# Rotary tables computed on folded tiles and spread through DRAM, with the softplus held in its place

## The chip, the cores and the metric

The kernel runs on one core of a Trainium2 chip. The metric is the device time of one execution in microseconds. The engines are named as in the profile: PE (matrix multiply; PEld is its weight load), DVE (vector), ACT (scalar functions and copies), POOL (not used here), SP (here it only issues DMAs). SBUF is the core's own memory with 128 partitions, PSUM holds the results of PE.

## The reference, cut to what matters

One layer of an encoder with 256 tokens and a model width of 2048. The normed input goes through one large projection. Its columns feed a latent attention (MLA) and a state space branch (SSD); both are gated, summed, projected, and followed by a gated feed-forward part. Two small pieces matter here: the rotary tables of the attention, and the softplus that makes the step sizes of the SSD.

```python
def rope_tables(positions):
    half = QK_ROPE_DIM // 2                      # 32 frequencies
    inv_freq = ROPE_THETA ** (-jnp.arange(half, dtype=jnp.float32) / half)
    ang = positions.astype(jnp.float32)[..., None] * inv_freq
    return jnp.cos(ang), jnp.sin(ang)

def apply_rope(x, cos, sin):
    x1, x2 = jnp.split(x.astype(jnp.float32), 2, axis=-1)
    return jnp.concatenate([x1 * cos - x2 * sin, x1 * sin + x2 * cos], axis=-1).astype(x.dtype)
...
    q_rope = apply_rope(q_rope, cos[:, :, None, :], sin[:, :, None, :])
    k_rope = apply_rope(k_rope, cos, sin)
...
    dt = jax.nn.softplus(dt_raw.astype(jnp.float32) + dt_bias.astype(jnp.float32))
```

## The kernel before

Activations lie with channels on the 128 partitions and the 256 tokens along the free axis. All projections are one list of jobs. A job multiplies a slab of 16 weight blocks (128 x 128 each, `raw`, three buffers, loaded by SP) with an activation. To keep float32 precision each half slab of 8 blocks is split in two: ACT makes the rounded part `wh` (L151), DVE the rest `wl` (L152), with five buffers each, so that the halves are made up to five ahead of PE (`HB=5`). PE multiplies `wh` with both parts of the activation in one matmul of 512 columns (L178, or L213 to L215 in jobs that give tokens on the partitions) and `wl` with the large part in 256 columns (L185).

The jobs at the start are: four slabs of the query latent `q` and four of the key/value latent `kv`, which use the unnormed input; then `kr` (the rotary key, from `krf`) and `dt` (the raw step sizes, `dtv`), which use the normed input `nHL` (tiles named xHL too, made in four quarters by `emit_n`: L314 on DVE scales, L290 on ACT and L291 on DVE split); a gate unit (L213 to L215, tiles `gate`); `R0` (the rotary part of the queries, from the normed latent `latH`/`latL`; matmuls L157 to L159); three gate units; `V0` (values, L573 to L575); `QK0`, and so on through the attention.

Small work is hung on the jobs by slot number with `at(slot, function)`. `rope_tables` is a generator whose steps are drawn a few at a time from slot 5 to 13. It computes, for all 128 partitions (each frequency four times, since the partitions hold two heads of two halves) and all 256 tokens, the angle, a long reduction of it to less than one turn (operations L337, L338, L341 in chains), the sine and the cosine (ACT, L366 and L367), and a sign by partition for the sine (L370). `swapped` exchanges the two halves of each head with four DMAs between SBUF tiles (`sw`, L377, issued by ACT), and `rotate` forms the rotated vector (L382 to L384). This happens once for `krf` and for each half of `R0` and `R1` (`rf`). `dt_softplus` is hung on slot 41. Of its instructions only the first, `nea` (L445), is kept in program order; the others may be moved earlier by the scheduler.

A scheduler of the tile framework sets the final order of each engine's instructions; each engine then runs its own list in order, and waits on semaphores. A DMA stands in the list of the engine that issues it. DMAs of SP and ACT count their completions on eight counters that the program hands out in turn: a DMA first waits until the earlier one on its counter has landed.

Of the kernel before, what the change touches and what calls it, by code (L numbers as in the profile page):

```python
# [8 lines left out]
F32 = mybir.dt.float32  # L9
F32R = mybir.dt.float32r  # L10
I32 = mybir.dt.int32
AF = mybir.ActivationFunctionType
ALU = mybir.AluOpType
AX = mybir.AxisListType

P = 128
S = 256
# [17 lines left out]
C_ID, C_U, C_L, C_INVF, C_SGN = 0, 128, 256, 384, 385  # L35
# [24 lines left out]
def tile_bidir_hybrid_layer(ctx: ExitStack, tc, xT, pos, vec, cst, w_in, w_r, w_v, w_qk, w_oa,  # L60
                            w_os, w_out, w_up, w_dn, out, RAWB=3, HB=5, NPG=29, NP1=18):
    nc = tc.nc
# [5 lines left out]
    dr = ctx.enter_context(tc.tile_pool(name="dr", bufs=1, space=bass.MemoryType.DRAM))  # L68

    act, dve, pe = nc.scalar, nc.vector, nc.tensor  # L70
# [4 lines left out]
    def p1(shape=(P, S), dt=F32, name="p1"):  # L75
        return pp.tile(list(shape), dt, tag="p1", bufs=NP1, name=name)
# [12 lines left out]
    CT = cp.tile([P, NCONST], F32, name="CT")  # L89
# [13 lines left out]
    def vcol(name, i=0):  # L103
        o = VOFF[name] + i
        return V[:, o:o + 1]
# [213 lines left out]


    rot = {}

    def rope_tables():

        cosT = rot["c"] = p1(name="cosT")
        sinT = rot["s"] = p1(name="sinT")
        pi_ = p1(dt=I32, name="posi")
        nc.scalar.dma_start(pi_, pos.broadcast_to([P, S]))
        a = p1(name="ang")
        q = p1(name="angq")  # L330
        qh = p1(name="angqh")
        t = p1(name="angt")
        k = p1(name="angk")
        MAGIC = 12582912.0

        def rounded(dst, src, scale):
            yield dve.tensor_scalar(dst, src, scale, MAGIC, ALU.mult, ALU.add)  # L337
            yield dve.tensor_scalar(dst, dst, MAGIC, None, ALU.subtract)  # L338

        def add_scaled(dst, src, c):  # L340
            yield dve.scalar_tensor_tensor(dst, src, c, dst, ALU.mult, ALU.add)  # L341

        def less_turns():
            yield from rounded(k, a, float(np.float32(1.0 / (2 * np.pi))))
            for c in TURN:
                yield from add_scaled(a, k, -c)


        yield dve.tensor_copy(a, pi_)
        yield dve.tensor_scalar(a, a, CT[:, C_INVF:C_INVF + 1], None, ALU.mult)  # L350
        yield from rounded(q, a, 2.0 ** -12)
        yield from add_scaled(a, q, -2.0 ** 12)
        yield from rounded(qh, q, 2.0 ** -10)
        yield from add_scaled(q, qh, -2.0 ** 10)
        yield dve.tensor_scalar(t, qh, TURN22[0], None, ALU.mult)
        yield from add_scaled(t, q, TURN12[0])
        yield from rounded(k, t, 1.0)
        yield dve.tensor_sub(t, t, k)
        yield from add_scaled(t, q, TURN12[1])
        yield from add_scaled(t, qh, TURN22[1])  # L360
        yield from less_turns()
        yield from add_scaled(a, t, 2 * float(np.pi))
        yield from less_turns()
        lim = float(np.nextafter(np.float32(np.pi), np.float32(0)))
        yield dve.tensor_scalar(a, a, lim, -lim, ALU.min, ALU.max)
        act.activation(sinT, a, AF.Sin)  # L366
        yield act.activation(cosT, a, AF.Sin, scale=0.5)  # L367
        yield dve.tensor_mul(cosT, cosT, cosT)
        yield dve.tensor_scalar(cosT, cosT, -2.0, 1.0, ALU.mult, ALU.add)
        yield dve.tensor_scalar(sinT, sinT, CT[:, C_SGN:C_SGN + 1], None, ALU.mult)  # L370

    def swapped(q, nb):

# [69 lines left out]
    def dt_softplus():  # L443
        v = dts["v"]
        tc.keep_in_program_order(act.activation(nea, vcol("alog"), AF.Exp))  # L445
        e, t, t2, o = p1(name="e"), p1(name="t"), p1(name="t2"), p1(name="o")
        act.activation(e, v, AF.Abs)
        act.activation(e, e, AF.Exp, scale=-1.0)
        dve.tensor_scalar(t, e, 2.0, None, ALU.add)
        dve.reciprocal(t, t)  # L450
        dve.tensor_mul(t, t, e)
        dve.tensor_mul(t2, t, t)
        n = 9
        dve.tensor_scalar(o, t2, 2.0 / (2 * n + 1), 2.0 / (2 * n - 1), ALU.mult, ALU.add)
        for k in range(n - 2, -1, -1):
            dve.tensor_mul(o, o, t2)
            dve.tensor_scalar(o, o, 2.0 / (2 * k + 1), None, ALU.add)
        dve.tensor_mul(o, o, t)
        dve.scalar_tensor_tensor(o, v, 0.0, o, ALU.max, ALU.add)
        dts["dt"] = o  # L460
        a = p1(name="a")
        dve.tensor_scalar(a, o, nea, -1.0, ALU.mult, ALU.mult)
        dts["a"] = a
# [525 lines left out]
    def at(slot, fn, *a):  # L989
        late.append((slot, lambda: fn(*a)))  # L990
# [14 lines left out]
    at(10, lat_norm, "kv")  # L1005
    at(13, lat_norm2, "kv", "kvn")
    steps = rope_tables()

    def rope_steps(n):
        for _ in range(n):  # L1010
            next(steps, None)

    for m in range(5, 14):
        at(m, rope_steps, 4 if m < 13 else 99)
    at(14, kr_rope)
    at(41, dt_softplus)
    at(46, dt_tokens)
    at(48, dt_cumsum)
# [67 lines left out]
    for g in range(G):  # L1086
# [9 lines left out]
        e, f = len(jobs) - b, 1  # L1096
# [205 lines left out]
```

## Time and profile before

| what | value |
|---|---|
| median of 3 runs | 1962.59 us (1961.36 to 1962.71) |
| the profiled execution | 1962.68 us, of which 1960.9 us from the first to the last instruction |
| PE busy | 1945.8 us (99%) |
| DVE busy | 1444.6 us (74%) |
| ACT busy | 1205.3 us (61%) |
| granted clock of PE | 0.998 |

In a timeline row the columns are start and duration in us, engine, line, operation, output and inputs, count, and in brackets the idle time of the engine ahead of it with what ended that. "x4" after a row means four instructions in a run, the duration being that of all. A row of `ACTq` or `SPq` is an instruction that only the engine's queue handles, such as the issue of a DMA. In the rows that group by line, the columns are the count, the busy time and the mean in ns of one, and the idle time before them.

### The profile page before, as it was taken

Reading aid. Unit: us, or ns where it says so; the run is one execution under the profiler, and the core shown is the slowest. Engines: PE = TensorE matmul, PEld = TensorE weight load, DVE = VectorE, ACT = ScalarE, POOL = GpSimd, SP = SyncE. Lnnn points to the kernel's source line nnn. Section 1 sums busy time; section 2 is a strip of 40 time slices with the busy share of each in tenths; the row PEclk is TensorE's granted clock in tenths of the full one; section 3 lists DMA queues with packets and bytes.
Section 4 is the critical chain, followed back from the end, with each engine's and each line's share of the span. In section 5 each row is a group of like instructions: output and inputs, shape, how many; then the busy total and the mean of one; then the engine's idle time right before and its main releaser. Section 6 shows DMA issues by size and latency. Waiting matters only on the chain.

```text
span 1960.9 us, 28920 instructions
## 1 busy us (share of the span) xinstructions
PE 1945.8 (99%) x11136; PEld 1707.2 (87%) x11136; DVE 1444.6 (74%) x2349; ACT 1205.3 (61%) x1878; POOL 0.2 (0%) x4
## 2 busy tenths in 40 slices
PE   9999999999999999999999999999999999999997
PEld 8889988888888888888888888888888888888887
DVE  7897744779779789879755566777656777557775
ACT  6566544687887887978644455666435655346553
POOL 0000000000000000000000000000000000000000
PEclk9999999999999999999999999999999999999999
DMA  7554456765665565565666665555555555555543
GB/s 279 179 173 154 137 172 216 251 222 172 215 233 173 198 234 194 194 215 182 205 196 198 200 222 176 190 193 192 181 189 190 194 192 175 194 192 193 188 161 124
DMA packets 93259, 379.31 MB, mean 193 GB/s; under 512 B 10688, under 2 KB 11328, under 8 KB 62912
## 3 DMA queue, kind: packets, MB, share of 16 engines
q1 hardware_dynamic: 91440, 375.09, 56.6%
q10 hardware_dynamic: 1680, 2.37, 0.4%
q8 instruction: 87, 1.43, 0.3%
q14 instruction: 52, 0.43, 0.1%
HBM read 371.91 MB, written 4.33 MB: 192 GB/s over the span
## 4 chain that ended last, share of the span: by engine, by line
PE 95%; DVE 3%; DMA 1%; ACT 1%; issue 0%; ACTq 0%; DVEq 0%; SPq 0%
PE g L178 42%; PE g L185 22%; PE g L214 7%; PE g L213 7%; PE g L215 7%; PE g L159 1%; PE g L157 1%; PE g L158 1%; DVE wl L152 1%; PE s L789 1%; PE s L798 1%; PE s L158 0%; PE s L159 0%; PE s L157 0%; PE s L771 0%; PE s L634 0%
## 5 line engine op out<-in xcount | busy, mean ns | idle before, releaser
L152 DVE TENSOR_TENSOR wl<-raw,wh 128x1024 fp32r<-128x1024 f32 (+1 forms) x670 | 802.7, 1209 | 328.1 <-ACT wh L151 181.3
L151 ACT ACTIVATE wh<-raw 128x1024 fp32r<-128x1024 f32 (+1 forms) x670 | 698.9, 1047 | 546.6 <-PE g L178 352.0
L178 PE MATMUL g<-xHL,wh 128*128 128x512 f32 x1424 | 341.7, 392 | 1.3 <-DVE xHL L291 1.1
L178 PE MATMUL g<-hHL,wh 128*128 128x512 f32 x1360 | 324.8, 391 | 0.0
L178 PEld LDWEIGHTS g<-xHL,wh 128*128 128x128 f32 x1424 | 262.4, 188 | 53.6 <-DVE xHL L291 1.5
L178 PEld LDWEIGHTS g<-hHL,wh 128*128 128x128 f32 x1360 | 249.8, 188 | 48.3
L185 PEld LDWEIGHTS g<-xHL,wl 128*128 128x128 f32 x1424 | 182.6, 191 | 7.0
L185 PE MATMUL g<-xHL,wl 128*128 128x256 f32 x1424 | 184.9, 283 | 0.0
L185 PEld LDWEIGHTS g<-hHL,wl 128*128 128x128 f32 x1360 | 174.3, 191 | 6.6
L185 PE MATMUL g<-hHL,wl 128*128 128x256 f32 x1360 | 176.4, 283 | 0.0
L178 PE MATMUL g<-aHL,wh 128*128 128x512 f32 x692 | 166.6, 391 | 0.1
L910 DVE SCALAR_TENSOR_TENSOR uc<-u,V,uc 128x255 f32<-128x255 f32 x176 | 85.3, 485 | 88.4 <-ACT uc L908 85.3
L178 PEld LDWEIGHTS g<-aHL,wh 128*128 128x128 f32 x692 | 126.9, 188 | 25.6 <-DVE aHL L928 1.3
L213 PE MATMUL g<-wh,yHL 128*128 128x512 f32 x256 | 100.1, 391 | 0.0
L214 PE MATMUL g<-wl,xHL 128*128 128x512 f32 x256 | 100.0, 391 | 0.0
L213 PE MATMUL g<-wh,xHL 128*128 128x512 f32 x256 | 100.0, 391 | 0.0
L215 PE MATMUL g<-wh,yHL 128*128 128x512 f32 x256 | 99.7, 389 | 0.0
L215 PE MATMUL g<-wh,xHL 128*128 128x512 f32 x256 | 99.6, 389 | 0.0
L214 PE MATMUL g<-wl,yHL 128*128 128x512 f32 x256 | 99.6, 389 | 0.0
L185 PEld LDWEIGHTS g<-aHL,wl 128*128 128x128 f32 x692 | 89.2, 191 | 3.6
L185 PE MATMUL g<-aHL,wl 128*128 128x256 f32 x692 | 90.4, 283 | 0.0
L684 DVE SCALAR_TENSOR_TENSOR xs<-cu,V,xs 128x254 f32<-128x254 f32 (+1 forms) x128 | 59.0, 479 | 0.2
(298 smaller groups left out, 2534.1 us busy)
## 6 DMA issues: line engine op xcount, KB each, us to landing
raw<-in_w_in SPq DMA_DIRECT2D x88, 1024.0 KB, 4.9
raw<-in_w_up SPq DMA_DIRECT2D x88, 1024.0 KB, 4.8
raw<-in_w_in SPq DMA_DIRECT2D x128, 256.0 KB, 3.9
raw<-in_w_os SPq DMA_DIRECT2D x128, 256.0 KB, 3.6
raw<-in_w_dn SPq DMA_DIRECT2D x32, 1024.0 KB, 5.0
raw<-in_w_oa SPq DMA_DIRECT2D x64, 256.0 KB, 3.9
FB<-acsD SPq DMA_DIRECT2D x32, 512.0 KB, 7.4
raw<-in_w_out SPq DMA_DIRECT2D x14, 1024.0 KB, 5.0
```

Source lines behind the costliest of these rows:

```text
L151: act.activation(vh, r, AF.Copy)
L152: dve.tensor_sub(vl, r, f32(vh))
L157: pe.matmul(ps, lhsT=wH, rhs=xH, start=first, stop=False)
L158: pe.matmul(ps, lhsT=wH, rhs=xL, start=False, stop=False)
L159: pe.matmul(ps, lhsT=wL, rhs=xH, start=False, stop=last)
L178: pe.matmul(ps, lhsT=wh[:, b, :], rhs=x, start=k == 0, stop=False)
L185: pe.matmul(cell["ps"][:, 0, :], lhsT=wl[:, b, :], rhs=get(k)[:, 0, :], start=False, stop=k == ktot - 1)
L213: pe.matmul(ps, lhsT=x[:, 0, ts], rhs=wH[:, kk, :], start=k == 0, stop=False)
L214: pe.matmul(ps, lhsT=x[:, 0, ts], rhs=wL[:, kk, :], start=False, stop=False)
L215: pe.matmul(ps, lhsT=x[:, 1, ts], rhs=wH[:, kk, :], start=False, stop=k == kt - 1)
L684: dve.scalar_tensor_tensor(o[:, a], u[:, b], vcol("cw", k * 48 + cb), o[:, a], ALU.mult, ALU.add)
L910: dve.scalar_tensor_tensor(o[:, a], u[:, b], vcol("fcw", k * 88 + cb), o[:, a], ALU.mult, ALU.add)
```

## The change

The tables are computed once per angle. There are 32 frequencies and 256 tokens; they are folded on the 128 partitions as four groups of 32 frequencies with 64 tokens each, so each operation has 64 columns instead of 256. Four DMAs load the positions of the four groups. The results (`tr`, cosine and sine) are stored with four DMAs in a DRAM tile `rotD` of 32 x 2 x 256 and loaded back with eight, four for the cosine table and four for the sine table, each to 32 partitions. The sign is applied to the sine after that, on 256 columns. The steps are drawn eight at a time from slot 5 to 10. The first operation of the softplus itself is also kept in program order.

```diff
     rot = {}
+    rotD = dr.tile([32, 2, S], F32, name="rotD")
 
     def rope_tables():
-        cosT = rot["c"] = p1(name="cosT")
-        sinT = rot["s"] = p1(name="sinT")
-        pi_ = p1(dt=I32, name="posi")
-        nc.scalar.dma_start(pi_, pos.broadcast_to([P, S]))
-        a = p1(name="ang")
...
-        k = p1(name="angk")
+        pi_ = p1((P, 64), I32, name="posi")
+        w = p1((P, 4, 64), name="ang")
+        a, q, qh, t = (w[:, i, :] for i in range(4))
+        k = p1((P, 64), name="angk")
+        tr = p1((P, 2, 64), name="trig")
+        cosT, sinT = tr[:, 0, :], tr[:, 1, :]
+        for c in range(4):
+            nc.scalar.dma_start(pi_[32 * c:32 * c + 32], pos[:, 64 * c:64 * c + 64].broadcast_to([32, 64]))
...
         yield dve.tensor_scalar(cosT, cosT, -2.0, 1.0, ALU.mult, ALU.add)
-        yield dve.tensor_scalar(sinT, sinT, CT[:, C_SGN:C_SGN + 1], None, ALU.mult)
+        for c in range(4):
+            nc.scalar.dma_start(rotD[:, :, 64 * c:64 * c + 64], tr[32 * c:32 * c + 32])
+        for i, nm in enumerate("cs"):
+            rot[nm] = p1(name="rot")
+            for c in range(4):
+                nc.scalar.dma_start(rot[nm][32 * c:32 * c + 32], rotD[:, i, :])
+        yield dve.tensor_scalar(rot["s"], rot["s"], CT[:, C_SGN:C_SGN + 1], None, ALU.mult)
...
-        act.activation(e, v, AF.Abs)
+        tc.keep_in_program_order(act.activation(e, v, AF.Abs))
...
-    for m in range(5, 14):
-        at(m, rope_steps, 4 if m < 13 else 99)
+    for m in range(5, 11):
+        at(m, rope_steps, 8 if m < 10 else 99)
```

The scheduler's order changes in three places; line numbers of the changed kernel are one higher than before up to the end of the tables and seven higher after them. Outside the first 110 us and the softplus, all engines keep their order.

First, ACT's list around the copy of the rotary key `krf`, before:

```order
L290 ACTIVATE xHL<-xw 128x512 x2
L151 ACTIVATE wh<-raw 128x1024
L237 ACTIVATE krf<-g 128x256
L377 DMA sw<-krf 32x256 x4
L419 ACTIVATE r_q<-s 128x256
L151 ACTIVATE wh<-raw 128x4x2x128
L439 ACTIVATE dtv<-g,V 128x256
L151 ACTIVATE wh<-raw 128x4x2x128
L424 ACTIVATE latH<-q 128x1024
L259 ACTIVATE rtok<-u,epsc 128x1 x2
```

and after:

```order
L372 DMA rotD<-trig 64x1x64 x4
L151 ACTIVATE wh<-raw 128x4x2x128
L376 DMA rot<-rotD 32x256 x8
L237 ACTIVATE krf<-g 128x256
L151 ACTIVATE wh<-raw 128x4x2x128
L384 DMA sw<-krf 32x256 x4
L426 ACTIVATE r_q<-s 128x256
L446 ACTIVATE dtv<-g,V 128x256
L259 ACT_TABLE_LOAD
L259 ACTIVATE rtok<-u,epsc 128x1
L431 ACTIVATE latH<-q 128x1024
```

The sine and cosine, with their table load, now come ahead of this piece (before, they stood behind it, between the DMAs of `rf`), the stores and loads of the tables stand ahead of the copy of `krf`, and a table load for the square root stands ahead of `rtok`.

Second, DVE's list from the last `kv` slab to the quarters of the normed input, before:

```order
L238 TENSOR_TENSOR kv<-kv,g 128x256
L314 TENSOR_TENSOR xw<-xw,r_x 128x1024
L402 TENSOR_TENSOR kvs<-kvs,sq_614 128x256
L314 TENSOR_TENSOR xw<-xw,r_x 128x1024
L291 TENSOR_TENSOR xHL<-xw,xHL 128x512 x2
L358 TENSOR_TENSOR angt<-angt,angk 128x256
L291 TENSOR_TENSOR xHL<-xw,xHL 128x512 x2
```

and after:

```order
L291 TENSOR_TENSOR xHL<-xw,xHL 128x512
L338 TENSOR_SCALAR angk<-ang 128x64
L409 TENSOR_TENSOR kvs<-kvs,sq_626 128x256
L339 TENSOR_SCALAR angk<-angk 128x64
L314 TENSOR_TENSOR xw<-xw,r_x 128x1024
L342 SCALAR_TENSOR_TENSOR ang<-angk,ang 128x64
L152 TENSOR_TENSOR wl<-raw,wh 128x4x2x128
L291 TENSOR_TENSOR xHL<-xw,xHL 128x512 x2
```

The last step before `krf` is one of the last reduction now (L342 with `angk`), where it was the middle of the first (L358); and the low half `wl` of the first gate unit stands ahead of the last quarter, where it stood behind it.

Third, DVE's list between the tables and `latL`, the small part of the query latent, after (before, these scalings of `q` by L422 stood among table steps, and the products of `krf` behind `latL`):

```order
L152 TENSOR_TENSOR wl<-raw,wh 128x4x2x128
L377 TENSOR_SCALAR rot<-rot,CT 128x256
L429 SCALAR_TENSOR_TENSOR q<-q,V,r_q 128x256 x4
L447 TENSOR_TENSOR dtv<-dtv,g 128x256
L389 TENSOR_TENSOR sw<-sw,rot 128x256
L390 TENSOR_TENSOR krf<-krf,rot 128x256
L391 TENSOR_TENSOR krf<-krf,sw 128x256
L432 TENSOR_TENSOR latL<-q,latH 128x1024
```

The sign on the loaded sine now stands ahead of the scalings of `q`, and the rotation of `krf` ahead of `latL`. The softplus, which stood on DVE among the first attention heads, now stands among the jobs of the attention's output projection.

More of the change, by code (lines that the diff above doesn't have):

```diff
@@ L321, in tile_bidir_hybrid_layer @@
     rot = {}
+    rotD = dr.tile([32, 2, S], F32, name="rotD")
     def rope_tables():
-        cosT = rot["c"] = p1(name="cosT")
-        sinT = rot["s"] = p1(name="sinT")
-        pi_ = p1(dt=I32, name="posi")
-        nc.scalar.dma_start(pi_, pos.broadcast_to([P, S]))
-        a = p1(name="ang")
-        q = p1(name="angq")
-        qh = p1(name="angqh")
-        t = p1(name="angt")
-        k = p1(name="angk")
+        pi_ = p1((P, 64), I32, name="posi")
[6 more added lines that the diff above has]
+            nc.scalar.dma_start(pi_[32 * c:32 * c + 32], pos[:, 64 * c:64 * c + 64].broadcast_to([32, 64]))
         MAGIC = 12582912.0
```

## The prediction

> **What bounds the kernel now.** I read the page's busy shares first, then the list of what PE waited for, then busy time by stretch.
>
> ```profile
> PE 1945.8 (99%) x11136; PEld 1707.2 (87%) x11136; DVE 1444.6 (74%) x2349; ACT 1205.3 (61%) x1878; POOL 0.2 (0%) x4
> ```
>
> ```profile
> PE g L178 <- DVE xHL L291: 1.1, 1, 1.1
> PE g L159 <- DVE wl L152: 1.1, 1, 1.1
> PE s L1168 <- DVE epsc L101: 1.0, 1, 1.0
> ...
> PE g L574 <- DVE wl L152: 0.3, 1, 0.3
> ```
>
> ```profile
> core 0: us, PE busy (x) PEld busy (x) DVE busy (x) ACT busy (x) POOL busy (x), PEclk, DMA share, GB/s
> 60.00:75.00 15.00, 13.90 (x80) 11.87 (x79) 14.85 (x31) 8.11 (x14) 0.00 (x0) 1.00 0.56 177
> 75.00:100.00 25.00, 25.00 (x136) 21.56 (x135) 19.93 (x36) 15.13 (x20) 0.00 (x0) 1.00 0.53 162
> 100.00:110.00 10.00, 8.62 (x56) 7.42 (x54) 9.80 (x14) 8.70 (x13) 0.00 (x0) 1.00 0.50 168
> 110.00:140.00 30.00, 29.99 (x208) 27.71 (x207) 29.00 (x56) 16.40 (x31) 0.00 (x0) 1.00 0.54 190
> 270.00:310.00 40.00, 40.00 (x181) 33.13 (x179) 19.85 (x18) 16.29 (x19) 0.00 (x0) 1.00 0.63 204
> ```
>
> The kernel is one long row of matmuls: PE is busy 1945.8 of 1960.9 us. The change takes no matmul away, so it can only shorten or lengthen PE's idle time. Where the tables are made and used, that is three waits, the two of 1.1 us and the one of 0.3, together 2.5 us, 0.13% of the time. That is the most it can gain. In these stretches DVE is full (14.85 of 15, 9.80 of 10), so DVE sets them. In 110 to 140, where the softplus runs now, DVE is as full (29.00 of 30) and PE still never stops (29.99).
>
> **Table arithmetic, on DVE.** 29 of the 30 operations go from 256 to 64 columns.
>
> ```profile
> L152 DVE TENSOR_TENSOR wl<-raw,wh 128x1024 fp32r<-128x1024 f32 x14 | 17.0, 1219 | 0.5 <-ACT wh L151 0.5
> L291 DVE TENSOR_TENSOR xHL<-xw,xHL 128x512 fp32r<-128x512 f32 x8 | 5.2, 683 | 0.0
> L314 DVE TENSOR_TENSOR xw<-xw,r_x 128x1024 f32<-128x1024 f32 x4 | 4.8, 1220 | 1.3 <-ACT r_x L311 1.3
> L341 DVE SCALAR_TENSOR_TENSOR ang<-angk,ang 128x256 f32<-128x256 f32 x6 | 2.5, 420 | 0.1
> L422 DVE SCALAR_TENSOR_TENSOR q<-q,V,r_q 128x256 f32<-128x256 f32 x4 | 1.7, 478 | 0.0
> L338 DVE TENSOR_SCALAR angk<-angk 128x256 f32<-128x256 f32 x3 | 0.9, 284 | 0.0
> L410 DVE TENSOR_TENSOR u<-s,rtok 128x1 f32<-128x1 f32 x4 | 0.4, 148 | 0.0
> ```
>
> These are DVE's groups from 42 to 90 us. 256 columns take 0.28 or 0.42 us, one column 0.15, so 64 take about 0.2 by a straight line. Operations in a row start about 0.08 us before the one ahead has ended (below, two L314 of 1.22 take 2.36). I count 0.12 us a step against 0.27 on average: 29 x 0.15 = 4.3 us off DVE. The ends are 0.07 (as one column) and 0.20 (as 256 columns of the cheaper kind).
>
> ```profile
> 42.20 2.36 DVE L314 TENSOR_TENSOR xw<-xw,r_x 128x1024 f32<-128x1024 f32 x2 [1.31 <-ACT r_x L311]
> 56.20 3.82 PE L178 MATMUL g<-xHL,wh 128*128 128x512 f32 x16
> 59.86 0.61 PE L213 MATMUL g<-wh,xHL 128*128 128x512 f32 x2
> 61.58 3.04 PE L178 MATMUL g<-xHL,wh 128*128 128x512 f32 x12 [1.10 <-DVE xHL L291]
> 64.46 2.08 PE L185 MATMUL g<-xHL,wl 128*128 128x256 f32 x16
> 66.37 1.09 PE L178 MATMUL g<-xHL,wh 128*128 128x512 f32 x4
> ...
> 101.53 0.50 PE L574 MATMUL g<-wl,latH 128*128 128x512 f32 x1 [0.28 <-DVE wl L152]
> 105.71 0.38 PE L159 MATMUL g<-latH,wl 128*128 128x256 f32 x1 [1.10 <-DVE wl L152]
> ```
>
> The three waits stand at 61.6, 101.5 and 105.7. PE's pace: 16 wide matmuls from 56.20 to 59.86, 0.229 us each; 16 narrow ones from 64.46 to 66.37, 0.119 each. Before, PE meets the third quarter of the normed input too early. In the new order the tables are run through by then (24 operations instead of 13), and PE does 24 wide matmuls and two of the first gate unit before it needs that unit's low half. DVE from 42.20 to that low half: six wl at 1.14, six xHL at 0.60, four L314 at 1.14, six 256-column additions at 0.34, six tiny ones at 0.075, 24 table steps at 0.12: 20.4 us, so 62.6, and PE goes on at 62.7. PE is there at 56.20 + 26 x 0.229 = 62.15. It waits 0.55 instead of 1.10: a gain of 0.55 (1.1 and a loss of 1.3 at the ends). What DVE has gained, it spends on running ahead.
>
> **The detour through DRAM, on ACT's queue.** It adds 15 DMAs there: three position loads, four stores, eight loads.
>
> ```profile
> 67.44 2.54 ACTq L377 DMA_DIRECT2D sw<-krf  x4
> 70.03 0.38 ACT L419 ACTIVATE r_q<-s 128x256 f32<-128x256 f32 x1 [3.07 <-PE g L185]
> 82.39 1.28 ACT L366 ACT_TABLE_LOAD   x1 [1.32 <-issue]
> 83.69 0.42 ACT L366 ACTIVATE sinT<-ang 128x256 f32<-128x256 f32 x1
> ```
>
> ```profile
> L377 ACTq DMA_DIRECT2D sw<-krf x4: 600/602/622, 67.4 to 69.4; - x4
> ...
> DMA to landing us min/median/max: 4.2/4.4/5.0
> ```
>
> ```profile
> L377 ACTq DMA_DIRECT2D sw<-rf x8: 514/623/752, 81.1 to 86.9; - x8
> ...
> DMA to landing us min/median/max: 2.0/4.9/7.2
> ```
>
> ```profile
> L502 SPq DMA_DIRECT2D acsD<-row x2: 326/378/430, 334.9 to 335.3; - x2
> ...
> DMA to landing us min/median/max: 2.9/3.0/3.1
> ```
>
> Issuing a DMA holds up ACT's own work: r_q's input from PE was there before 69, and r_q started at 70.03, when the four issues that stand ahead of it (2.54 us) were over. An issue between SBUF tiles takes 0.60, one to DRAM 0.38; I take 0.38 for the new ones. The extra position loads cost about 1.1 us at 41.5, hidden since the next weight half that ACT makes there is used at 56.2. The others are not only issues: the loads wait for the stores to land, and the last two of the eight for the landing of the first, because the program counts completions on eight counters in turn and two DMAs of one counter may not be under way together. I take 3.0 us for a store (nearest row: acsD, SBUF to DRAM) and 4.5 for a load (krf rows, same size, same moment, same weight traffic); the ends are 2.0 and 7.2.
>
> By these: PE frees the buffer of the weight half that stands between stores and loads at 62.7 + 18 x 0.229 + 32 x 0.119 + 0.25 = 70.9, ACT has made it at 71.9, the stores have landed at 71.6. The loads start at 72.0. The first lands at 76.5, the last two are then issued and ACT's queue is free at 77.3. Behind it stand the copy krf (0.3), a weight half (1.0, done 78.6), the four sw DMAs (78.1 to 80.5) and r_q (80.9).
>
> **R0's inputs.** Before, R0 had its latents without a wait. Now DVE must sign the sine (its load issued 76.9, landed 81.4, signed 81.7) ahead of the four scalings of q (4 x 0.40, to 83.35), and ACT makes latH at 84.4. PE, without a wait since 62.7, has 42 more wide and 32 narrow ones by 76.1, then 24 wide and 0.83 us of small ones: it wants latH at 82.45. It waits 1.95. After two matmuls it wants the weight half that ACT makes behind latH (85.6): 0.95. After two more it wants latL, which on DVE stands behind the three products of krf, and these behind sw's landing (79.9 + 4.5 = 84.4, products 85.45, latL 86.7): 0.65. Together 3.55.
>
> The new order also has one table load more, on ACT between dtv and rtok, at 81.3 to 82.5; latH is held longer by DVE, so it costs nothing here. The row has 1.28 us and the sine starting 1.30 after it. The Trainium skill (ScalarE: Activation LUTs, What ACT_TABLE_LOAD costs) adds a drain and puts a switch at 2.66 us. By that latH would be 0.8 later and the sum 3.8; the row here shows no such drain.
>
> **V0 and after.** The waits of 0.3 and 1.1 us stood on DVE's rotation of rf, which waits for sw's landing; that stays, and R0 now ends nearer to V0. The tables' arithmetic is gone from DVE before it. I leave the 1.4 us as they are (bounds: gone, or 3 more if a landing takes 7.2).
>
> **The softplus.**
>
> ```profile
> L469 PE MATMUL s<-CT,o x2: 271/272/272, 309.6 to 309.7; 128*128 128x128 f32 x2
> ```
>
> It moves from 105 to 140 us to about 285. PE lost nothing at the old place, and at the new one DVE has 20 of 40 us free for its 10, with weight halves made five ahead. Its results are used by PE at 309. Nothing either way; without that cover it would be at most the reciprocal's length, under 2 us.
>
> **Sum.** -0.55 + 3.55 + 0 = +3.0 us on the profiled execution's 1962.68, which lies 0.1 above the median of 1962.59: 1965.6.
>
> **Rivals.** *Hidden.*
>
> ```profile
> L132 SPq DMA_DIRECT2D raw<-in_w_in x4: 328/424/430, 57.8 to 59.2; - x4
> ...
> DMA to landing us min/median/max: 3.0/3.6/3.9
> ```
>
> Landings near 2.0 us, as the fastest sw row. Then the last load is held by a weight load on its counter instead (issued at 71.4, when the second store has landed, and landing some 3.7 later, as these rows have it) and goes out at 75.1, latH is done at 82.65 (wait 0.2), the next half 0.95 late, latL in time: 1.15 - 0.55 = +0.6, 1963.2. If V0's waits go as well, 1961.8; with all three gone, 1960.1. Against it: none of the four krf DMAs at that moment landed under 4.2. The Trainium skill (DMA: Bandwidth & Descriptors, Anatomy of one DMA) fits 2.0 us plus bytes over 436 GB/s for the GpSimd path, 2.1 us for 32 KB, which would make this rival the result; the krf rows are twice that.
>
> *Clearly slower.* The landings follow one another (first load, then the sine's load, and in parallel sw), so each us more in one landing is about two in the sum. At 7.2 the queue is free at 80.0, the sine signed at 87.1, latH done at 89.8, latL at 92.1: waits 7.35, 0.95 and 0.7, +8.4, 1971.0. From 4.95 us a landing on it passes 0.2%. For it: rf's eight have median 4.9, and krf's longest is 5.0. Against it: the krf median 4.4.
>
> *No effect from the softplus's place, or a loss:* above, within 2 us, and inside the forecast.
>
> **How the numbers follow.** 0.2% (3.9 us) is about what a measurement of this kernel can tell from no change. Forecast, +1 to +3.9: 0.42. Hidden, -2.5 to +1: 0.20. Clearly slower, above +3.9: 0.35. Something that I do not see gains more than the 2.5 us: 0.03. So faster 0.03, same 0.62, slower 0.35. The range runs from V0's waits gone with quick landings (rounded to 1961) to the end with slow ones (1971).
>
> **What would show it.** PE's wait at 61.6 falls to about half. A new wait of PE on latH, L157, of about 2 us near 82, then one on a weight half and one on latL. ACT idle from 72 to 77 behind the loads of rot, and r_q some 10 us later than at 70.03. The table operations of 64 columns near 0.2 us. DVE in 110 to 140 no longer full, with PE as full as before. The prediction is wrong if rot lands in 2 us or in 7, or if ACT runs on past a DMA that waits.

## The result and the profile after

The changed kernel takes 1970.01 us (median of 5, 1969.79 to 1970.81), the kernel before 1962.59 (median of 5): ratio 1.004, 95% interval 1.0025 to 1.0054. It is slower by 7.4 us, 0.38%, where +3.0 was forecast. The profiled execution has a span of 1968.0 us against 1960.9.

The same five stretches as in the prediction, of the changed kernel (four shown):

```profile
core 0: us, PE busy (x) PEld busy (x) DVE busy (x) ACT busy (x) POOL busy (x), PEclk, DMA share, GB/s
60.00:75.00 15.00, 14.39 (x79) 12.20 (x78) 11.00 (x19) 6.90 (x9) 0.00 (x0) 1.00 0.55 177
75.00:100.00 25.00, 20.87 (x111) 17.12 (x110) 13.27 (x27) 10.05 (x15) 0.00 (x0) 0.93 0.53 168
100.00:110.00 10.00, 9.13 (x40) 6.92 (x39) 8.66 (x14) 7.93 (x11) 0.00 (x0) 1.00 0.19 37
110.00:140.00 30.00, 28.21 (x188) 25.47 (x187) 24.41 (x34) 18.85 (x31) 0.00 (x0) 1.00 0.62 209
```

Read PE's busy time against its column of before. 60 to 75 gains 0.5 us. 75 to 100, which PE crossed without a gap, now has 4.13 us of idle time, and its granted clock is 0.93, which is about 25 x 0.07 = 1.7 us more. 100 to 140 loses 1.3 us more than before. That makes 6.6 of the 7.1 us of span. DVE has done less work in each of these stretches and is full in none: the loss is not DVE's.

What ACT did from 68 to 88 us, row by row (start, length, operation, idle time ahead of it and what ended it):

```profile
68.49 2.62 ACTq L372 DMA_DIRECT2D rotD<-trig  x4
71.16 1.06 ACT L151 ACTIVATE wh<-raw 128x1024 fp32r<-128x1024 f32 x1 [2.59 <-PE g L215]
74.41 7.12 ACTq L376 DMA_DIRECT2D rot<-rotD  x8
81.58 0.38 ACT L237 ACTIVATE krf<-g 128x256 f32<-128x256 f32 x1 [9.36 <-DMA rot<-rotD]
81.86 1.05 ACT L151 ACTIVATE wh<-raw 128x1024 fp32r<-128x1024 f32 x1
82.45 2.48 ACTq L384 DMA_DIRECT2D sw<-krf  x4
84.98 0.38 ACT L426 ACTIVATE r_q<-s 128x256 f32<-128x256 f32 x1 [2.07 <-DMA sw<-krf]
85.26 0.47 ACT L446 ACTIVATE dtv<-g,V 128x256 f32<-128x256 f32 x1
85.74 1.28 ACT L259 ACT_TABLE_LOAD   x1
87.04 0.29 ACT L259 ACTIVATE rtok<-u,epsc 128x1 f32<-128x1 f32 x1
87.24 1.04 ACT L431 ACTIVATE latH<-q 128x1024 fp32r<-128x1024 f32 x1
```

From 72.2 to 81.6 ACT computes nothing: 9.36 us behind the loads. The next fences are lines of the stores' view (L372), the last line of the loads' view (L376), and three rows of timelines: SP's load of the first weight slab of `V0`, 1 MB, and the loads' last issues.

```profile
L372 ACTq DMA_DIRECT2D rotD<-trig x4: 609/618/683, 68.5 to 70.5; - x4
...
DMA to landing us min/median/max: 3.6/3.9/4.2
```

```profile
DMA to landing us min/median/max: 2.7/6.5/7.7
```

```profile
74.39 0.33 SPq L134 DMA_DIRECT2D raw<-in_w_v  x1
...
77.69 0.44 ACTq L376 DMA_DIRECT2D rot<-rotD  x1
80.75 0.78 ACTq L376 DMA_DIRECT2D rot<-rotD  x2
```

The last store goes out at 70.5 and lands near 74.3; only then does the first load go. Six loads are out by 78.1. The seventh has the first one's counter and stands until 80.75, 6.3 us after the first was issued. PE, in order of time:

```profile
62.70 0.50 PE L214 MATMUL g<-wl,xHL 128*128 128x512 f32 x1 [0.61 <-DVE wl L152]
...
82.96 0.50 PE L213 MATMUL g<-wh,xHL 128*128 128x512 f32 x1 [2.92 <-ACT wh L151]
84.22 0.50 PE L214 MATMUL g<-wl,xHL 128*128 128x512 f32 x1 [0.76 <-DVE wl L152]
...
85.55 0.63 PE L213 MATMUL g<-wh,xHL 128*128 128x512 f32 x1
85.97 0.63 PE L214 MATMUL g<-wl,xHL 128*128 128x512 f32 x1
...
88.33 0.70 PE L157 MATMUL g<-latH,wh 128*128 128x256 f32 x2
89.46 0.74 PE L213 MATMUL g<-wh,xHL 128*128 128x512 f32 x2 [0.43 <-ACT wh L151]
...
108.22 0.50 PE L581 MATMUL g<-wl,latH 128*128 128x512 f32 x1 [0.83 <-DVE wl L152]
112.55 0.39 PE L157 MATMUL g<-latH,wh 128*128 128x256 f32 x1 [1.77 <-ACT gate L667]
```

PE stands still for the weight half that ACT makes at 81.86, behind the loads. Then, from 85.5, matmuls that wait for nothing come every 0.43 us instead of every 0.23: the clock.

### The profile page after: what moved, and what is told of

Read it like the earlier page. It is cut to its first block, busy times and chain, and to the rows that moved or that the text cites. A ratio compares the mean times of both kernels' runs of the same rounds, so it can differ in the third digit from the quotient of the medians.

```text
span 1968.0 us, 28935 instructions
## 1 busy us (share of the span) xinstructions
PE 1948.4 (99%) x11136; PEld 1708.7 (87%) x11136; DVE 1441.8 (73%) x2349; ACT 1205.9 (61%) x1879; POOL 0.2 (0%) x4
## 4 chain that ended last, share of the span: by engine, by line
PE 94%; DVE 2%; ACT 2%; DMA 1%; issue 0%; ACTq 0%; SPq 0%; DVEq 0%
PE g L178 42%; PE g L185 22%; PE g L213 7%; PE g L214 7%; PE g L215 7%; PE g L157 1%; PE g L158 1%; PE g L159 1%; PE s L796 1%; PE s L805 1%; DVE wl L152 1%; ACT wh L151 1%; PE s L159 0%; PE s L158 0%; PE s L157 0%; DMA sw<-rf 0%
## 5 line engine op out<-in xcount | busy, mean ns | idle before, releaser
L213 PEld LDWEIGHTS g<-wh,xHL 128*128 128x128 f32 x256 | 48.2, 189 | 13.2 <-ACT wh L151 4.0
```

What stands on the lines that cost most here:

```text
L213: pe.matmul(ps, lhsT=x[:, 0, ts], rhs=wH[:, kk, :], start=k == 0, stop=False)
```

## The experiments

Theory Q: the loss is ACT's in-order queue, which the detour holds from 68.5 to 81.6. Its rivals change from run to run and stand in the expectations. Ratios are against the kernel before on the same chip (1961.9 to 1962.2).

| run | median us | ratio | 95% interval |
|---|---|---|---|
| pin alone | 1962.31 | 1.0001 | 0.9992 to 1.0009 |
| folded, no detour | 1962.53 | 1.0002 | 0.9993 to 1.0011 |
| detour on ACT, loads read by nobody | 1970.35 | 1.0043 | 1.0030 to 1.0055 |
| detour on POOL | 1970.93 | 1.0046 | 1.0033 to 1.0058 |
| detour on POOL, read by nobody | 1967.41 | 1.0028 | 1.0017 to 1.0039 |
| four loads, ACT | 1967.79 | 1.0029 | 1.0018 to 1.0041 |
| four signed loads, ACT | 1967.63 | 1.0027 | 1.0018 to 1.0036 |
| four signed loads, POOL | 1964.28 | 1.0012 | 1.0003 to 1.0021 |
| the same, one position DMA | 1960.90 | 0.9996 | 0.9987 to 1.0005 |
| rot in large tiles, ACT | 1968.17 | 1.0032 | 1.0020 to 1.0045 |
| without the pin | 1970.29 | 1.0042 | 1.0028 to 1.0056 |
| four signed, one position, ACT | 1965.24 | 1.0017 | 1.0008 to 1.0026 |

**Pin alone, and the change without it.** The first is the kernel before with

```
-        act.activation(e, v, AF.Abs)
+        tc.keep_in_program_order(act.activation(e, v, AF.Abs))
```

> The kernel before, with only the softplus's first operation pinned to its place. Theory Q (the loss is ACT's in-order queue, held from 68.5 to 81.6 us by the detour's stores and loads): the softplus does nothing, 1962.6, within 1 us. Rival S (the softplus's new place costs: PE's longer waits near 108 and 112 us come from it): 1963.5 to 1965.

The second is the changed kernel with that line taken back.

> The changed kernel without the softplus's pin: the order puts it back near 115 to 140 us. Theory: the pin is worth nothing here either, 1969.5 to 1970.5. Rival (with the tables' arithmetic gone, the pin gains or loses): a difference of over 1 us from the changed kernel's 1970.0.

1962.31 and 1970.29: the softplus's place costs and gains nothing that these runs can tell, in either kernel, and rival S falls.

**Folded, without the detour.**

```
-        for c in range(4):
-            nc.scalar.dma_start(rotD[:, :, 64 * c:64 * c + 64], tr[32 * c:32 * c + 32])
...
+        rot["c"], rot["s"] = cosT, sinT
...
+            v = t.rearrange("p n (c k) -> p (n c) k", k=64)
+            dve.tensor_mul(v, v, r.unsqueeze(1).broadcast_to([P, 4 * nb, 64]))
```

> The changed kernel without the detour: no store, no load; the rotation reads the folded tables of 64 columns four times over, so the spread of the angles is left out and the rotated values are not those of the reference. Theory Q: all of the loss is the detour, and what is left is the folding's gain at the first wait, of which the forecast made 0.55 us: 1962.0, between 1960 and 1963. Rival F (the folded order itself, with its extra table load on ACT and the new places of the steps, costs): 1965 or more.

1962.53: the loss is gone with the detour, so rival F falls. But there is no gain either. The chain to the first low half is shorter, and PE's wait there is 0.40 us, yet the waits at `V0` have grown instead:

```profile
63.57 0.50 PE L214 MATMUL g<-wl,xHL 128*128 128x512 f32 x1 [0.40 <-DVE wl L152]
98.94 0.50 PE L577 MATMUL g<-wh,latL 128*128 128x512 f32 x1 [0.27 <-DVE latL L427]
103.67 0.50 PE L576 MATMUL g<-wl,latH 128*128 128x512 f32 x1 [1.72 <-DVE wl L152]
```

**The detour on ACT, read by nobody.** The run above, with the four stores and eight loads put back (into tiles that nothing reads).

> As the changed kernel, with its four stores and eight loads on ACT's queue, but nobody reads what the loads bring: the rotation reads the folded tables as in the run without a detour (same part left out). Theory Q: DVE no longer waits for the sine's landing, and still nearly all of the loss stays, because ACT's queue is held all the same: 1969 to 1970.5. Rival L (the loss is the landing itself, as the forecast's chain had it: sine landed, signed, q scaled, latH): the loss goes, 1962 to 1965.

1970.35, all of the loss. Here no operation reads the loaded tables, and PE's longest wait is the same one:

```profile
82.83 0.50 PE L213 MATMUL g<-wh,xHL 128*128 128x512 f32 x1 [2.82 <-ACT wh L151]
```

So holding ACT's queue is enough, and rival L falls for this kernel.

**The detour on POOL.**

```
-            nc.scalar.dma_start(rotD[:, :, 64 * c:64 * c + 64], tr[32 * c:32 * c + 32])
+            nc.gpsimd.dma_start(rotD[:, :, 64 * c:64 * c + 64], tr[32 * c:32 * c + 32])
...
-                nc.scalar.dma_start(rot[nm][32 * c:32 * c + 32], rotD[:, i, :])
+                nc.gpsimd.dma_start(rot[nm][32 * c:32 * c + 32], rotD[:, i, :])
```

> The changed kernel with the four stores and eight loads issued by POOL, which does nothing else there, instead of ACT. Theory Q: ACT runs on; DVE may still wait a little for the sine (stores landed near 73, loads near 80, wanted by 82): 1962 to 1965. Rival L (landing, not queue): 1967 to 1970, since the way through DRAM is as long as before.

A miss: 1970.93, nearer to what rival L said. ACT is free (it starts `latH` at 79.66), but the same wait now stands in DVE's list:

```profile
84.34 0.35 DVE L377 TENSOR_SCALAR rot<-rot,CT 128x256 f32<-128x256 f32 x1 [5.07 <-DMA rot<-rotD]
84.61 0.15 DVE L418 TENSOR_TENSOR u<-u,rtok 128x2 f32<-128x2 f32 x1
84.68 1.22 DVE L152 TENSOR_TENSOR wl<-raw,wh 128x1024 fp32r<-128x1024 f32 x1
85.82 1.21 DVE L432 TENSOR_TENSOR latL<-q,latH 128x1024 fp32r<-128x1024 f32 x1
```

```profile
87.09 0.39 PE L158 MATMUL g<-latL,wh 128*128 128x256 f32 x1 [4.45 <-DVE latL L432]
```

The sine's sign waits for the landing; `latL`, which does not need it, stands behind it, and PE waits 4.45 us. All that follows comes later, too: the copies of rf go out at 93.09, and at `V0` PE waits another 2.77 us. With one in-order queue freed, the next one in the way holds.

**On POOL, read by nobody.** The third run with `nc.gpsimd` in the stores and loads.

> The detour on POOL's queue again, but nobody reads what the loads bring (the rotation reads the folded tables, so the spread of the angles is left out). Theory Q+L (the detour costs in two in-order queues: ACT's, because it issues and waits, and, once ACT is free, DVE's, because the sine's sign operation waits for the landing ahead of latL): both are free here, 1962 to 1963.5. Rival T (the transfers themselves, by their traffic and by the completion counters that they share with the weight loads, slow the rest): 1966 or more, as neither queue is freed from that.

1967.41, a miss, and not a clean run: the sign works in place on the tile that the stores read, and so waits for their landing (2.40 us on DVE, with r_q and so 1.24 us of PE behind it), and the order still has `krf` and r_q late. The larger wait comes at `V0`, 2.74 us: the copies of rf go out at 88.26, and DVE makes the low weight half that PE needs there behind the rotation, which waits for them. The time is in rival T's range, and this run leaves that rival open; the runs that follow part its two halves, traffic and counters.

**Where the tiles come from.** The two loaded tables taken from the pool of large tiles, all else as in the change:

```
-            rot[nm] = p1(name="rot")
+            rot[nm] = page([P, S], name="rot")
```

> The changed kernel with the two rot tiles out of the pool of large tiles instead of the small one; eight loads on ACT, sign on DVE, all as in the change. The order then has krf, r_q and dtv ahead of the loads and of a weight half more behind them. Theory Q: ACT is held as long (stores 68.5, loads from 74, copies of krf whose counters are those of loads): latH near 83 to 85 where PE wants it near 79.5; 1968 to 1970. Rival O (the loss was that r_q stood behind the loads): 1963 to 1966.

1968.17, as theory Q has it. This alone lets the scheduler put `krf`, r_q and dtv ahead of the loads (why it did not before wasn't traced further), and gains 1.8 us; PE then waits 4.40 us on `latH`, which still stands behind the loads.

**Four loads instead of eight, and the sign put on before.**

```
-            for c in range(4):
-                nc.scalar.dma_start(rot[nm][32 * c:32 * c + 32], rotD[:, i, :])
+        cs = page([P, 2, S], name="rot")
+        for c in range(4):
+            nc.scalar.dma_start(cs[32 * c:32 * c + 32], rotD[:, :, :])
```

> The changed kernel with four loads of both tables in place of eight, into one tile of the large pool; still on ACT. The order then has r_q and krf ahead of the loads, but latH still behind them and behind the four copies of krf, and the sign on DVE still ahead of latL. Theory Q+L: the queue is held less, though a copy of krf shares its counter with the first load (landing near 81), so latH is done at 82 to 83.5 and latL some 2 us later: 1964 to 1967. Rival N (the number of loads and the place of r_q do not matter, the way through DRAM does): 1969 or more.

The second of the two adds

```
+        yield dve.tensor_scalar(tr[:, 2, :], sinT, -1.0, None, ALU.mult)
...
-        yield dve.tensor_scalar(rot["s"], rot["s"], CT[:, C_SGN:C_SGN + 1], None, ALU.mult)
```

and loads the sine or its negative, by block.

> As the run with four loads on ACT, and the sign is put on ahead of the detour: a third folded table, minus the sine, is stored as well, and each block of 32 rows loads the sine or its negative. So no operation of DVE but the rotation itself waits for the landing, and the order has that behind latL. Theory Q+L: only ACT's queue is left, 1963.5 to 1966. Rival: same as with the sign on DVE, if the sign never was what latL waited for.

1967.79 and 1967.63, both above the forecast, and the sign is worth nothing that can be told while ACT is held. What holds it in the second, beside the loads (1.78 us), is the four copies of krf behind them, 4.62 us instead of 2.5 by waits for their counters:

```profile
74.49 1.78 ACTq L376 DMA_DIRECT2D rot<-rotD  x4
76.36 4.62 ACTq L384 DMA_DIRECT2D sw<-krf  x4
81.03 1.06 ACT L431 ACTIVATE latH<-q 128x1024 fp32r<-128x1024 f32 x1 [7.87 <-DMA sw<-krf]
```

**The same on POOL.**

> The same with the stores and the four loads on POOL's queue: ACT holds no DMA of the detour, and DVE needs the tables only behind latL. The whole function is computed. Theory Q+L: as without any detour, 1962 to 1963.5. Rival T (traffic and counters): 1965 or more.

1964.28, 0.8 above the forecast. `latH` starts at 74.46, and PE crosses 75 to 95 without a wait. What is left comes later, on ACT again, and PE waits 1.84 and 0.64 us at `V0`:

```profile
85.07 7.61 ACTq L384 DMA_DIRECT2D sw<-rf  x4
92.73 0.38 ACT L426 ACTIVATE r_kv<-s 128x256 f32<-128x256 f32 x1 [6.74 <-issue]
```

Four copies of rf need some 2.5 us elsewhere, and 7.6 here. In the program the third of them takes the counter of the weight load that SP issues at 86.79 and that lands 4.7 us later. Each DMA that a change adds on SP's or ACT's queue shifts every later one there to another of the eight counters. The change added 15 to them. This version adds three, those of the position: in its trace POOL's eight DMAs count on eight semaphores of their own (110 to 117).

**One position DMA,** so that the detour adds none to the eight counters of SP and ACT, and these fall as before:

```
-        for c in range(4):
-            nc.scalar.dma_start(pi_[32 * c:32 * c + 32], pos[:, 64 * c:64 * c + 64].broadcast_to([32, 64]))
+        nc.scalar.dma_start(pi_, pos.rearrange("o (c k) -> c o k", c=4).broadcast_to([4, 32, 64]))
```

> The run with four signed loads on POOL, and the position brought by one DMA in place of four, so that the detour adds eight DMAs to the program and each DMA behind it falls on the completion counter that it had before the change. Theory C (what was left there, +2.2 us, is a copy of the second rf on ACT that shares its counter with a weight load of 1 MB issued at 86.8 and so held ACT until 92.7): the copy now shares with a weight load that landed long before, ACT is not held, 1962 to 1963. Rival (the detour's traffic, or the order alone): 1964 or more, as before. The whole function is computed.

(The expectation counts POOL's eight DMAs as well; eight are one full turn, so it comes to the same.) 1960.90, below the forecast, with the whole function computed. The second four copies of rf, from 84.78, take 2.62 us, nothing is held, and the two waits that are left in this part are 0.6 us each, where the kernel before had 1.10, 0.28 and 1.10:

```profile
PE g L178 <- DVE xHL L291: 0.6, 1, 0.6
PE g L159 <- DVE wl L152: 0.6, 1, 0.6
```

The bytes moved are those of the run before, so the traffic half of rival T falls; its other half, the shared counters, is what this run bears out. Ten of its eleven runs lie between 1960.69 and 1961.51, below all 21 of the kernel before (1961.63 to 1962.82), but the interval of the ratio, 0.9987 to 1.0005, holds 1: a gain of about 1 us is likely and not shown.

**The same on ACT.**

> The run with one position DMA, but stores and the four loads on ACT in place of POOL. Theory Q: ACT's queue alone: latH behind the loads' wait for the stores and the copies of krf, so PE waits 2 to 3 us on it, and a copy of rf shares its counter with the weight load issued near 87: 1965.5 to 1968.5. Rival (with counters put right, ACT's queue carries the detour for nothing): 1962 to 1964.

1965.24, 4.3 us above the run on POOL with nothing else changed: PE waits 2.34 us on `latH`, then 0.63 on a weight half. From 81.2 the granted clock is 0.50 for 3.4 us besides, 1.7 us of work. So the steps from the change down are: large tiles 1.8, four loads 0.4, the sign 0.2, one position DMA 2.4, ACT's queue 4.3 us. The 0.4 and 0.2 lie within the scatter of their runs. The 2.4 is not the counters' alone: in this run SP's 1 MB load for `V0` goes out only at 82.45, where it went at 75.00 with four position DMAs on ACT, and the four table loads, issued from 74.55 to 76.36, land in a third of the time (5.1 to 7.2 us there, L376). The scheduler moved some other rows with the position's DMA, too, here and on POOL. SP's row and the loads' view of this run:

```profile
82.45 0.33 SPq L134 DMA_DIRECT2D raw<-in_w_v  x1
```

```profile
L375 ACTq DMA_DIRECT2D rot<-rotD x4: 353/440/465, 74.6 to 75.9; - x4
...
DMA to landing us min/median/max: 1.9/2.1/2.2
```

So here ACT is held no longer by slow loads, but by the loads' wait for the stores and by the issues. The sizes belong to this order of steps: with ACT freed first, DVE's wait took the loss over.

## Why the prediction was right, and where not

The time fell inside the range, but on the side of the rival *clearly slower* (chance 0.35), not on the likeliest case, which had less than half of the loss. The path was right: stores and loads in ACT's list, and PE's waits behind it at `R0`. By its steps:

- **First wait, 1.10 to 0.55.** Held: 0.61, and PE goes on at 62.70 where 62.7 was worked out. The 64-column operations take about 0.2 us (0.19 to 0.23 in the rows), with 0.10 to 0.13 from one start to the next.
- **The most to be gained, 2.5 us.** Held as a bound: the run without a detour gained nothing, the best version about 1.
- **ACT's queue, the step that failed in size.** Each of its three prices was low. A store's issue was put at 0.38 us and took 0.62. Its landing was put at 3.0 and took 3.9. The stores also began at 68.49, where 71.6 for their landing goes back to the copies' old start, 67.44. So the loads went out at 74.4, not 72.0. A load's landing was put at 4.5 and took 6.5 (the first one 6.3). The queue was free at 81.6 instead of 77.3 and r_q came at 84.98 instead of 80.9. The row for the loads was chosen by size and moment (krf's copies). As far as these runs tell, it was the wrong one by what was under way beside it: krf's copies went out among weight loads of 256 KB, the table loads beside the 1 MB load of 74.39, which took 8.4 us to land. In the last run of the list, with that load 8 us later, table loads of twice the size landed in 2.1.
- **The whole, by the prediction's own rate.** That rate, two us in the sum for one in a landing, gives 3.0 + 2 x 2.0 = 7.0 for the 6.5 measured, and the span grew by 7.1. That the two are so close is in part luck: around `R0` the rows show 4.1 us of waits and 1.7 of half clock, 2.3 more than forecast and not 4.0, and the rest came at `V0` and from half a us outside these stretches. Half clock is in no term of the sum.
- **PE's waits.** Forecast: 1.95 on `latH`, 0.95 on a weight half, 0.65 on `latL`. Measured: 2.92 on the weight half *ahead* of `latH` (forecast done at 78.6, made at 82.9), 0.76 on its low part, 0.43 on another; `latH`, 88.3 instead of 84.4, ended just as PE came to it, because PE's clock was down.
- **Extra table load, at nothing.** Held: it ran at 85.74 while DVE scaled q, and its next operation started 1.30 us after it, with no drain. The 2.66 us that the Trainium skill gives (ScalarE: Activation LUTs, What ACT_TABLE_LOAD costs) were not to be seen.
- **`V0` unchanged.** No: 0.83 + 1.77 where 0.28 + 1.10 stood, 1.2 us more, inside the bounds that were given. The second wait has another end than before, ACT's `gate` (L667) and not a weight half of DVE. ACT is late there; one cause in its rows is that the second four copies of rf took 3.99 us, where four took 2.56 before. No run takes that apart.

```profile
97.96 3.99 ACTq L384 DMA_DIRECT2D sw<-rf  x4
```

- **Softplus, at nothing.** Held, in two runs.
- **Hidden.** Refuted as a forecast of this kernel: no store landed under 3.6 us, and the loads' median was 6.5, where 2.0 was needed. The 2.1 us for 32 KB, an estimate by the fit that the Trainium skill (DMA: Bandwidth & Descriptors, Anatomy of one DMA) gives for the GpSimd path, are far under this trace, where weight loads share the DMA engines. The last run, with 2.1 us for loads of 64 KB, shows that such landings do occur here, but not beside the 1 MB load.
- **The counters.** The prediction used them for the loads' last two only. It did not count that 15 added DMAs move all later ones to other counters; the runs with one position DMA gained 2.4 us on ACT, with quicker landings besides, and 3.4 on POOL, there with the held copies seen to go free.

## What to carry to other kernels

A DMA that waits on another DMA does not belong in the queue of an engine that has work for the critical path, and the first consumer of what it brings does not belong ahead of such work either: look at every in-order list that the wait passes through, since freeing one only shows the next. Price a landing by rows with the same transfers under way beside them, not by those of the same size. Where completions are counted on a few shared counters, count the DMAs that a change adds to that set, and see which transfers each later one then waits behind.

## What the runs showed of the hardware

Where PE paused long enough, the granted clock fell to 0.50 and stayed there for 3.4 us or for twice that. It fell 2.2 to 5.4 us after the pause had begun, in some runs still within a pause, in others when PE was at work again. Changed kernel, PE's pause from 80.04 (busy time, granted clock, DMA share, GB/s for each us):

```profile
core 0: us, PE busy (x), PEclk, DMA share, GB/s
85.00:86.00 1.00, 1.00 (x5) 0.69 0.24 57
86.00:87.00 1.00, 1.00 (x4) 0.50 0.00 0
87.00:88.00 1.00, 1.00 (x4) 0.50 0.00 0
88.00:89.00 1.00, 0.98 (x3) 0.60 0.00 0
89.00:90.00 1.00, 0.57 (x3) 1.00 0.00 0
```

Four signed loads on POOL, pause from 97.3:

```profile
99.00:100.00 1.00, 0.49 (x1) 0.84 0.00 0
100.00:106.00 6.00, 5.69 (x13) 0.50 0.23 53
106.00:107.00 1.00, 1.00 (x5) 0.74 0.98 418
```

A clock of 0.69 over 1 us is 0.62 us at half speed, and so on: 0.62 + 1 + 1 + 0.80 = 3.42 us in the first, 0.32 + 6 + 0.52 = 6.84 in the second, twice as long. Each 3.42 us cost PE 1.7 us of work. In the changed kernel most of that lay where PE would have waited for `latH` in any case; in the second it was a plain loss, more than the 1.84 and 0.64 us of waiting ahead of it. In the first 120 us of the profiled executions, every wait of 2.34 us or more was followed by half clock (for 6.8 us after 4.40 with large tiles, for 3.4 after 4.45 with the detour on POOL), and no wait of up to 1.77 us that stood alone was (1.72 in folded, no detour; 1.77 at `V0` in the changed kernel). The second profile is of an execution of 1965.54 us, where that kernel's median is 1964.28; how long half clock lasts in the others is not known. The Trainium skill (TensorE: Matmul & The Clock Gate, Part 1: The HAM clock gate) tells of a window of about 3.4 us, at half clock after an idle one; the lengths agree with the trace, but pauses well under 3.4 us were enough here. The prediction priced waits of PE by their length alone; for the waits of over 2 us here that was too little.
